# First weights and p in smaller pieces on two DMA queues, a Newton step for 1/f, and the last stores cut otherwise, in a one-core decoder block

## The chip, the cores and the metric

The kernel runs on one core of one Trainium2 chip. A core has five engines that run side by side, each through its own list of instructions in order: TensorE (PE, matmuls; its weight loads are shown apart as PEld), VectorE (DVE), ScalarE (ACT), GpSimd (POOL) and SyncE (SP), which here only issues DMAs. ScalarE issues a few DMAs too. The metric is the device time of one execution in microseconds (us); the kernel before takes 826.49 us in the median of three runs (826.37 to 826.64).

## What is computed

One layer of a decoder block over 256 tokens of 2048 features, in float32. Cut to what matters (weights of a kind in one letter):

```
h  = rmsnorm(x)
u  = h @ w_in                                  # 12288 columns, split into
c, b, xa, za, q, fl, iv, og, ga, gb            # gates and values
ya = b * conv3(c * xa) * silu(za)              # short convolution, 1024 wide
o  = gated recurrence of (silu(q), (1-lb)*sigmoid(-fl), iv, log f), 8 heads of 128
yb = rmsnorm_per_head(o) * silu(og)
m  = sigmoid(ga) * (ya @ w_a) + sigmoid(gb) * (yb @ w_b)
x  = x + m @ w_o
x  = x + sigmoid(rmsnorm(x) @ w_pg) * (p @ w_pp)    # p is 256 x 256
out = rmsnorm(x)
```

## The kernel before, in words

**Matmuls in three parts.** Every large product is done as three matmuls in a fast float32 format: a number is split into a high part (rounded, made by ScalarE) and a low part (the rest, made by VectorE), and high x high, high x low and low x high are summed. `split` does that for weights: ScalarE writes `whi` (L124), VectorE `wlo` (L125). `put` does it for x (L197, L198), and `put_p` for p (L897 the copy to the high part, on VectorE; L898 the low part). All three matmuls are at L945 in `product`.

**Stream of weights.** The weights are one stream of positions. Each position is 128 partitions x 1024 columns (512 KB): two slices of 128 rows, each against 512 output columns. A position gives 12 matmuls: two slices, two halves of the tokens, three parts. The first four positions are the product of p with `w_pp` (groups "PP", one position each, 512 output columns each); then come 16 groups of `w_in` of eight positions, the gates with `w_a` and `w_b`, then `w_o`, and last `w_pg`. The main loop runs over the positions; before the matmuls of a position it splits positions up to three ahead (`LEAD`), loads are issued four further ahead, and after the matmuls it advances the epilogues. Four buffers hold split weights, three hold raw ones of two positions each. Python generators hold the epilogues: each `yield` ends a portion, and the loop runs one portion of each active epilogue per position. Where a portion stands decides the order of instructions on each engine; within an engine nothing overtakes.

**The start.** At L154 the whole of p (256 KB) is loaded on SP's queue. `load_first` (L106 to L111) loads position 0 in two halves of 512 columns, one on ScalarE's queue and one on SP's, and position 1 in one DMA. Then follow the small parameters `prm_t` (L158), and positions 2 to 5 mixed with pieces of x (L810). Ten matmuls on a tile of zeros, which VectorE clears first (L821), run at L825 before any weights are there. In the loop, position 0 is split by halves, each preceded by `put_p` of its 128 rows of p; the first half's six matmuls go high x high, low p, low weights, so that they can begin before the low parts are made. Evictions of the PP groups are at L713, and their stores are put off.

**The recurrence.** `hgrn(j)` runs twice (j = 0, 1; about 100 to 185 us and 300 to 365 us). It builds a decay-masked product of queries and keys by levels of blocks: factors on VectorE, ScalarE (exponentials) and GpSimd, many small matmuls (`products`, L389, and L520), and masked copies (`keep`, copy_predicated) from PSUM into the tiles `both` and `a`. For the innermost level of two rows it makes f = exp(b_r - b_l) on ScalarE (L500) and 1/f by two reciprocals of 256 columns on VectorE (L501, L503), multiplies keys by 1/f on VectorE (L509) and queries by f on GpSimd (L510), and copies `both` into `a` under a mask (L511), twice. Products with the values are at L542 to L544.

**The convolution.** `ep_xa` turns its input through DRAM (`turned`), then for four tiles of features does one scaled copy on ScalarE (L608) and seven fused multiply-adds on VectorE (L617), spread over portions. Its result is used by `ep_b`.

**The end.** The last group of `w_pg` is done by token halves, the last half of tokens in two pieces of 256 columns. After the last matmul come the sigmoid, product, sum and squares (`last_half`, L747 to L752), the norm factor r on GpSimd (L773), the scaling of 2048 columns in four quarters (ScalarE L778, two quarters; VectorE L780 and L782, one each), and a store per quarter (L785; one on ScalarE's queue, three on SP's).

**What orders the work around the change.** SP issues its DMAs in program order, and a DMA waits on a semaphore that is shared with an earlier one (eight in turn). `tc.issue_after` places an instruction behind a named one in its engine's list. Nothing else reorders.

Of the kernel before, what the change touches and what calls it, by code (L numbers as in the profile page):

```python
# [9 lines left out]
F32 = mybir.dt.float32  # L10
# [5 lines left out]
P = 128  # L16
T = 256
# [6 lines left out]
CW = 512  # L24
PLE = 256
EPS = 1e-6
WARM = 10
LB_FLOOR = 1e-30
LB_MAX = 1.0 - 1e-6
SCAN = 64  # L30
# [14 lines left out]
def hybrid_kernel(ctx, tc, xT, x, pT, prm, gfin, masks, w_in, w_a, w_b, w_o, w_pg, w_pp, out):  # L45
# [57 lines left out]
                nc.sync.dma_start(out=raw, in_=w[g, :, c : c + 2, :])  # L103
        return loaded[pos // 2]

    def load_first(pos, queues):  # L106

        w, g, c = stream[pos]
        n = 2 * CW // len(queues)
        for i, eng in enumerate(queues):  # L110
            eng.dma_start(out=load(pos)[:, pos % 2, i * n : (i + 1) * n], in_=w[g, :, c, i * n : (i + 1) * n])  # L111

    def split(pos, halves=(0, 1)):
        w, g, c = stream[pos]
        src = load(pos)[:, pos % 2, :]

        pool, n = (pools["late"], 6) if (pos - state.get("late", len(steps))) % 10 < 6 and "late" in state else (wp, 4)
        if pos not in parts:
            parts[pos] = tuple(
                pool.tile([P, 2 * CW], F32R, tag=tag, bufs=n, name=nm(tag)) for tag in ("whi", "wlo")  # L120
            )
        hi, lo = parts[pos]
        s = slice(halves[0] * CW, (halves[-1] + 1) * CW)
        a = nc.scalar.activation(out=hi[:, s], in_=src[:, s], func=AF.Copy)  # L124
        v = nc.vector.tensor_tensor(  # L125
            out=lo[:, s], in0=src[:, s], in1=hi[:, s].bitcast(F32), op=ALU.subtract
        )
        state["splits"] = (a.ins, v.ins)
# [22 lines left out]
    FIRST = 6  # L151

    praw = t4()[:, : 2 * T]
    nc.sync.dma_start(out=praw.rearrange("p (k t) -> p k t", k=2), in_=pT)  # L154
    load_first(0, (nc.scalar, nc.sync))
    load_first(1, (nc.sync,))
    prm_t = const.tile([P, PRM_N], F32, name="prm_t")
    nc.sync.dma_start(out=prm_t, in_=prm)  # L158

    if PAD_CONST:  # L160
        nc.gpsimd.memset(const.tile([P, PAD_CONST], F32, name="pad"), 0.0)
# [189 lines left out]
    def hgrn(j):  # L351
# [122 lines left out]
        for i in range(4):  # L474
            keep(both, 2 + i, heads(bk), 32 * i)
        Xs.append(level(LEVELS[1]))
        yield
        yield
        yield

        e = t4()
# [10 lines left out]
        nc.vector.tensor_tensor(out=X[:, 0], in0=ev[:, :, 0], in1=kv[:, :, 0], op=ALU.mult)  # L492
        nc.gpsimd.tensor_tensor(out=X[:, 1], in0=ev[:, :, 1], in1=qv[:, :, 1], op=ALU.mult)

        f, rf = (t4()[:, :512] for _ in range(2))
        bl, br = halves(b, 2)
        nc.vector.tensor_tensor(
            out=f.rearrange("p (n c) -> p n c", c=1), in0=br, in1=bl, op=ALU.subtract
        )
        nc.scalar.activation(out=f, in_=f, func=AF.Exp)  # L500
        nc.vector.reciprocal(out=rf[:, :256], in_=f[:, :256])  # L501
        yield
        nc.vector.reciprocal(out=rf[:, 256:], in_=f[:, 256:])  # L503
        yield
        k2, q2 = tiles(kT, 2), tiles(qT, 2)
        fv, rv = (z.rearrange("p (h k n) -> p h k n", h=4, k=2) for z in (f, rf))
        for blk in range(2):
            kk, qq = k2[:, :, blk, :, 1 - blk, 0], q2[:, :, blk, :, 1 - blk, 0]
            nc.vector.tensor_tensor(out=kk, in0=kk, in1=rv[:, :, blk], op=ALU.mult)  # L509
            nc.gpsimd.tensor_tensor(out=qq, in0=qq, in1=fv[:, :, blk], op=ALU.mult)  # L510
            nc.vector.copy_predicated(  # L511
                out=a[:, blk],
                mask=mask_t[:, len(LEVELS) + blk : len(LEVELS) + blk + 1, :].to_broadcast([P, 4, P]), data=both,
            )
        yield
        yield
        bo = bank("s")
# [75 lines left out]
    def ep_xa(j, psum):  # L593
        cx = t4()
        plain_times(psum, state["c", j], cx)
        cxT = yield from turned(cx, 4)
        cv = t4("cv", 1)
        for h in range(2):
            for i in range(2):
                n = h * 2 + i  # L600
                k = j * 4 + n
                d, s = cv[:, n * T : (n + 1) * T], cxT[:, n * T : (n + 1) * T]

                def w(tap):
                    c = PRM_CONV + tap * 8 + k
                    return prm_t[:, c : c + 1]

                nc.scalar.activation(out=d, in_=s, func=AF.Identity, scale=w(2))  # L608

                for tap, to, fr, n_ in (  # L610
                    (1, 1, 0, P - 1), (1, P, P + 1, P - 1), (1, T - 1, P - 1, 1),
                    (0, 2, 0, P - 2), (0, P, P + 2, P - 2), (0, T - 2, P - 1, 1), (0, T - 1, P - 2, 1),
                ):
                    if (tap, to) == (0, 2):
                        yield
                        yield
                    nc.vector.scalar_tensor_tensor(  # L617
                        out=d[:, to : to + n_], in0=s[:, fr : fr + n_], scalar=w(tap), in1=d[:, to : to + n_],
                        op0=ALU.mult, op1=ALU.add,
                    )  # L620
                if n < 3:
                    yield
                    yield
        state["cv", j] = cv

    def ep_za(j, psum):
# [142 lines left out]
    def last_norm(t):  # L769

        xs, r, tot = state["x"], sc(1, "r3", 2), state["tot3", t]
        nc.vector.tensor_tensor(out=tot, in0=tot, in1=state["ss3"][:, t * 6 + 4 : t * 6 + 5], op=ALU.add)
        nc.gpsimd.tensor_tensor(out=r, in0=tot, in1=mhalf[:, :1], op=ALU.pow)  # L773
        for q in (2, 0, 3, 1):
            s = slice(q * CW, (q + 1) * CW)
            d = xs[:, t, s]
            if q < 2:
                nc.scalar.activation(out=d, in_=d, func=AF.Identity, scale=r)  # L778
            elif q == 2:
                nc.vector.tensor_scalar(out=d, in0=d, scalar1=r, scalar2=None, op0=ALU.mult)  # L780
            else:
                nc.vector.scalar_tensor_tensor(  # L782
                    out=d, in0=d, scalar=r, in1=state["gfin"][:, s], op0=ALU.mult, op1=ALU.mult
                )
            (nc.scalar if q == 1 else nc.sync).dma_start(out=out[:, t, s], in_=d)  # L785

    def ep_last(t, halves):

# [24 lines left out]
        )  # L813

    for c in range(4):
        load_first(c + 2, (nc.sync,))
        load_x(c)


    warm = pools["tmp1"].tile([P, 4, P], F32, tag="both", bufs=1, name="warm")  # L820
    nc.vector.memset(warm[:, :2, :], 0.0)  # L821
    warm = warm[:, :2, :].rearrange("p h t -> p (h t)").bitcast(mybir.dt.bfloat16)
    wb = bank("s")
    for _ in range(WARM):
        nc.tensor.matmul(wb, warm[:, :P], warm, start=True, stop=True)  # L825

    def put_x(k):
        put(state["hT"], k, xraw[k // 4][:, (k % 4) * T : (k % 4 + 1) * T], gain(PRM_GMIX, k))
# [119 lines left out]
    for pos, (gi, c) in enumerate(steps[:last_group]):  # L948
# [8 lines left out]

            order.enter_context(tc.issue_after(state["evicted"]))
        while done < min(pos + 1 + ahead(pos), len(steps)):
            if done == 0:  # L960
                for i in range(2):
                    put_p(i)
                    split(done, (i,))
            else:
                for k in range(2 * (done - 4), min(2 * (done - 4) + 2, KT)) if done >= 4 else ():
                    put_x(k)
                split(done)
            done += 1
        order.close()
        if 2 <= pos < 6:  # L970
# [13 lines left out]
        hi, lo = parts.pop(pos)  # L984
        for i in range(2):
            k = 2 * c + i
            s = slice(i * CW, (i + 1) * CW)
            for n in ((0,), (2,), (1,)) if pos == 0 and i == 0 else ((0, 1, 2),):
                for t in range(NT):
                    product(psum[t], state[opname], k, t, hi[:, s], lo[:, s], k == 0, k == 2 * nch - 1, n)  # L990


        if kind == "PG" and j == 0 and c < 2:
# [130 lines left out]
```

## Time and profile before

| | |
|---|---|
| time, median of 3 runs | 826.49 us (826.37 to 826.64) |
| profiled execution, its own time | 827.48 us |
| its span, first to last instruction | 825.0 us |
| TensorE clock granted, mean | 0.996 |
| TensorE busy | 814.1 us, 99% |
| VectorE / ScalarE / GpSimd busy | 533.1 / 431.6 / 86.8 us |
| DMA | 187.25 MB, 227 GB/s mean |
| first useful matmul, first x matmul, last matmul | 5.36, 17.05, 815.67 us |

How to read it: times in the views are microseconds from the start of the span. A row of the timeline gives start, busy time, engine, line, operation, tiles written and read, and in brackets how long the engine stood idle before it and what ended that. A row of the waits gives who waited for whom, the total, how often and the longest. "issue" is idle time for which the profile shows no cause. SPq, ACTq and PEq are the engines' sequencers, which issue DMAs and handle semaphores. The ends of matmuls are modelled, so the distance between starts says more than the busy time.

### The profile page before, as it was taken

The page shows a single profiled execution, that of the slowest core. Times are in us where ns is not written, and L with a number is a line of the kernel's source. Part 1 is how long each engine was busy: PE and PEld are TensorE (multiplying, and loading weights), DVE is VectorE, ACT ScalarE, POOL GpSimd, SP SyncE. Part 2 cuts the span into 40 slices and gives each one's busy share as a digit, 9 for nine tenths or more (in the row PEclk, how much of TensorE's full clock was granted, in tenths as well). Part 3 has the DMA queues.
Part 4 walks back from the last instruction along what each step waited for, and adds up shares of the span by engine and source line. Part 5 has one row for each costly group of instructions (what it writes and reads, how often), then busy time and mean ns, then how long its engine had stood idle before and what let it go on. Part 6 is the DMA issues. An engine that isn't in the chain of part 4 may idle for free.

```text
span 825.0 us, 10664 instructions
## 1 busy us (share of the span) xinstructions
PE 814.1 (99%) x4186; PEld 674.1 (82%) x4186; DVE 533.1 (65%) x616; ACT 431.6 (52%) x555; POOL 86.8 (11%) x74
## 2 busy tenths in 40 slices
PE   9999999999999999999999999999999999999995
PEld 6888888888888888888888888888888888888885
DVE  5747698966766598977645546545544656679633
ACT  7667465455564465466443543544444455566522
POOL 1000045200000064100001001000100000001210
PEclk9999999999999999999999999999999999999998
DMA  9969656648776664748555755756755787887702
GB/s 340 371 262 339 219 189 207 209 154 263 245 235 226 205 205 160 249 155 286 200 185 186 264 187 174 253 202 204 245 182 192 248 293 274 303 301 269 292 1 103
DMA packets 40659, 187.25 MB, mean 227 GB/s; under 512 B 4640, under 2 KB 13856, under 8 KB 22432
## 3 DMA queue, kind: packets, MB, share of 16 engines
q1 hardware_dynamic: 40176, 185.78, 65.8%
q10 hardware_dynamic: 432, 0.79, 0.3%
q8 instruction: 32, 0.52, 0.2%
q14 instruction: 19, 0.16, 0.1%
HBM read 172.92 MB, written 13.63 MB: 226 GB/s over the span
## 4 chain that ended last, share of the span: by engine, by line
PE 96%; issue 1%; DMA 1%; DVE 0%; ACT 0%; SPq 0%; POOLq 0%; POOL 0%
PE g L945 94%; PE s L945 1%; PE s L389 1%; DMA raw<-in_w_pp 1%; PE s L520 0%; PE s L544 0%; PE s L543 0%; PE s L542 0%; ACT xs L778 0%; DVE wlo L125 0%; ACT whi L124 0%; DVE t L748 0%; DVE t L752 0%; DVE xs L751 0%; POOLq L1119 0%
## 5 line engine op out<-in xcount | busy, mean ns | idle before, releaser
L125 DVE TENSOR_TENSOR wlo<-raw,whi 128x1024 fp32r<-128x1024 f32 (+1 forms) x293 | 365.5, 1253 | 252.3 <-ACT whi L124 251.5
L124 ACT ACTIVATE whi<-raw 128x1024 fp32r<-128x1024 f32 (+1 forms) x293 | 307.6, 1056 | 334.4 <-PE g L945 291.9
L945 PE MATMUL g<-whi,xh 128*128 128x512 f32 (+1 forms) x912 | 351.8, 387 | 0.5 <-issue 0.5
L945 PE MATMUL g<-wlo,xh 128*128 128x512 f32 (+1 forms) x912 | 351.9, 386 | 0.0
L945 PE MATMUL g<-whi,xl 128*128 128x512 f32 (+1 forms) x912 | 351.8, 386 | 0.0
L945 PEld LDWEIGHTS g<-whi,xh 128*128 128x128 f32 x912 | 171.4, 188 | 35.0 <-issue 1.0
L945 PEld LDWEIGHTS g<-whi,xl 128*128 128x128 f32 x912 | 171.4, 188 | 34.4
L945 PEld LDWEIGHTS g<-wlo,xh 128*128 128x128 f32 x912 | 171.5, 188 | 34.0
L945 PE MATMUL g<-whi,mh 128*128 128x512 f32 x128 | 49.8, 390 | 0.0
L945 PE MATMUL g<-wlo,mh 128*128 128x512 f32 x128 | 49.7, 390 | 0.0
L945 PE MATMUL g<-whi,ml 128*128 128x512 f32 x128 | 49.6, 390 | 0.0
L672 POOL TENSOR_TENSOR t<-ga,gb 128x512 f32<-128x512 f32 x6 | 10.6, 1788 | 198.1 <-DVE gb L667 198.1
L945 PEld LDWEIGHTS g<-whi,mh 128*128 128x128 f32 x128 | 24.0, 188 | 5.2 <-ACT mh L678 0.3
L945 PEld LDWEIGHTS g<-whi,ml 128*128 128x128 f32 x128 | 24.0, 188 | 5.1 <-DVE ml L679 0.2
L945 PE MATMUL g<-whi,yaTh 128*128 128x512 f32 x72 | 28.1, 395 | 0.0
L945 PE MATMUL g<-wlo,yaTh 128*128 128x512 f32 x72 | 28.0, 391 | 0.1
L945 PEld LDWEIGHTS g<-wlo,mh 128*128 128x128 f32 x128 | 24.0, 188 | 4.9
L945 PE MATMUL g<-whi,yaTl 128*128 128x512 f32 x72 | 27.9, 390 | 0.0
L443 POOL TENSOR_TENSOR t<-b 128x512 f32<-128x512 f32 x10 | 20.4, 2036 | 68.2 <-DVE b L319 41.1
L945 PE MATMUL g<-whi,ybTl 128*128 128x512 f32 x64 | 24.9, 389 | 0.0
L945 PE MATMUL g<-whi,ybTh 128*128 128x512 f32 x64 | 24.9, 389 | 0.0
L945 PE MATMUL g<-wlo,ybTh 128*128 128x512 f32 x64 | 24.9, 389 | 0.0
(156 smaller groups left out, 515.3 us busy)
## 6 DMA issues: line engine op xcount, KB each, us to landing
raw<-in_w_in SPq DMA_DIRECT2D x93, 1024.0 KB, 5.0
raw<-in_w_o SPq DMA_DIRECT2D x16, 1024.0 KB, 5.3
raw<-in_w_pg SPq DMA_DIRECT2D x16, 1024.0 KB, 5.8
turn<-t SPq DMA_DIRECT2D x72, 128.0 KB, 2.6
t<-turn SPq DMA_DIRECT2D x18, 512.0 KB, 5.1
raw<-in_w_a SPq DMA_DIRECT2D x8, 1024.0 KB, 5.2
raw<-in_w_b SPq DMA_DIRECT2D x8, 1024.0 KB, 5.1
raw<-in_w_in SPq DMA_DIRECT2D x6, 512.0 KB, 7.8
```

The costliest lines, as they stand in the source:

```text
L124: a = nc.scalar.activation(out=hi[:, s], in_=src[:, s], func=AF.Copy)
L125: v = nc.vector.tensor_tensor(out=lo[:, s], in0=src[:, s], in1=hi[:, s].bitcast(F32), op=ALU.subtract)
L389: nc.tensor.matmul(heads(bk)[r, h, c if at is None else slice(at, at + 32)], key(h)[:, r], query(h)[:, c], start=True, stop=True, tile_pos ...
L443: nc.gpsimd.tensor_tensor(out=er, in0=br, in1=ref, op=ALU.subtract)
L672: (nc.vector if j == 3 else nc.gpsimd).tensor_tensor(out=spread(m, t), in0=blocks(ga[:, s]), in1=blocks(gb[:, s]), op=ALU.add)
L945: nc.tensor.matmul(psum, a, b, start=first and n == 0, stop=last and n == 2)
```

## The change

It does six things.

1. p's two tiles are loaded by a DMA each (128 KB): the first on SP's queue, the second on ScalarE's.
2. Position 0's first 512 columns come as two pieces of 256 columns on ScalarE's queue, ahead of p's second tile; the other 512 columns on SP's; position 1 as two halves on SP's. `prm_t` is loaded later, behind position 2. The splits follow these pieces (`EARLY`), the first half's matmuls run by 256 columns, and `put_p` of the second tile is placed behind the splits of the first two pieces.
3. The warm-up matmuls are 7 and not 10, on a constant of ones that exists already, so VectorE clears no tile for them.
4. In `hgrn`, 1/f is no reciprocal any more: ScalarE makes exp(-(b_r - b_l)), and VectorE improves it by one Newton step, r (2 - f r), in a product and a fused operation with the sign reversed; the sign is put right where the keys are multiplied. The two masked copies of `both` into `a` move to earlier portions.
5. In `ep_xa` two portions more pass before the convolution, and fewer between its tiles.
6. In `last_norm` VectorE scales 256, 512 and 256 columns and not 512 and 512; SP stores 256, 512 and 512 columns, ScalarE one piece of 768.

On TensorE the order of everything behind the first six matmuls is as before. There are 3 pairs of weight load and matmul fewer (warm-ups) and 6 pairs more (the pieces), and two instructions more that wait for a second semaphore.

The diff, cut to its core:

```
@@ -24,7 +24,9 @@
 CW = 512
 PLE = 256
 EPS = 1e-6
-WARM = 10
+WARM = 7
+EARLY = {0: ((0, CW // 2), (CW // 2, CW), (CW, 2 * CW)), 1: ((0, CW), (CW, 2 * CW))}
 LB_FLOOR = 1e-30
 LB_MAX = 1.0 - 1e-6
 SCAN = 64
@@ -103,14 +105,7 @@
                 nc.sync.dma_start(out=raw, in_=w[g, :, c : c + 2, :])
         return loaded[pos // 2]
 
-    def load_first(pos, queues):
-        w, g, c = stream[pos]
-        n = 2 * CW // len(queues)
-        for i, eng in enumerate(queues):
-            eng.dma_start(out=load(pos)[:, pos % 2, i * n : (i + 1) * n], in_=w[g, :, c, i * n : (i + 1) * n])
-    def split(pos, halves=(0, 1)):
+    def split(pos, c0=0, c1=2 * CW):
         w, g, c = stream[pos]
         src = load(pos)[:, pos % 2, :]
 
@@ -120,7 +115,7 @@
                 pool.tile([P, 2 * CW], F32R, tag=tag, bufs=n, name=nm(tag)) for tag in ("whi", "wlo")
             )
         hi, lo = parts[pos]
-        s = slice(halves[0] * CW, (halves[-1] + 1) * CW)
+        s = slice(c0, c1)
         a = nc.scalar.activation(out=hi[:, s], in_=src[:, s], func=AF.Copy)
         v = nc.vector.tensor_tensor(
             out=lo[:, s], in0=src[:, s], in1=hi[:, s].bitcast(F32), op=ALU.subtract
@@ -151,11 +146,22 @@
     FIRST = 6
 
     praw = t4()[:, : 2 * T]
-    nc.sync.dma_start(out=praw.rearrange("p (k t) -> p k t", k=2), in_=pT)
-    load_first(0, (nc.scalar, nc.sync))
-    load_first(1, (nc.sync,))
+    def load_p(k, eng=nc.sync):
+        eng.dma_start(out=praw[:, k * T : (k + 1) * T], in_=pT[:, k, :])
+    def load_columns(pos, c0, c1, eng):
+        w, g, c = stream[pos]
+        eng.dma_start(out=load(pos)[:, pos % 2, c0:c1], in_=w[g, :, c, c0:c1])
+    load_p(0)
+    load_columns(0, 0, CW // 2, nc.scalar)
+    load_columns(0, CW // 2, CW, nc.scalar)
+    load_p(1, nc.scalar)
+    load_columns(0, CW, 2 * CW, nc.sync)
+    for n in range(2):
+        load_columns(1, n * CW, (n + 1) * CW, nc.sync)
     prm_t = const.tile([P, PRM_N], F32, name="prm_t")
-    nc.sync.dma_start(out=prm_t, in_=prm)
 
     if PAD_CONST:
         nc.gpsimd.memset(const.tile([P, PAD_CONST], F32, name="pad"), 0.0)
@@ -474,8 +480,9 @@
         for i in range(4):
             keep(both, 2 + i, heads(bk), 32 * i)
         Xs.append(level(LEVELS[1]))
-        yield
-        yield
+        for blk in range(2):
+            yield
+            keep(a[:, blk], len(LEVELS) + blk, both)
         yield
 
         e = t4()
@@ -492,26 +499,27 @@
         nc.vector.tensor_tensor(out=X[:, 0], in0=ev[:, :, 0], in1=kv[:, :, 0], op=ALU.mult)
         nc.gpsimd.tensor_tensor(out=X[:, 1], in0=ev[:, :, 1], in1=qv[:, :, 1], op=ALU.mult)
 
-        f, rf = (t4()[:, :512] for _ in range(2))
+        fr, one = t4(), t4()[:, :512]
+        f, rf = fr[:, :512], fr[:, 512:]
         bl, br = halves(b, 2)
         nc.vector.tensor_tensor(
             out=f.rearrange("p (n c) -> p n c", c=1), in0=br, in1=bl, op=ALU.subtract
         )
+        nc.scalar.activation(out=rf, in_=f, func=AF.Exp, scale=-1.0)
         nc.scalar.activation(out=f, in_=f, func=AF.Exp)
-        nc.vector.reciprocal(out=rf[:, :256], in_=f[:, :256])
-        yield
-        nc.vector.reciprocal(out=rf[:, 256:], in_=f[:, 256:])
+        yield
+        nc.vector.tensor_tensor(out=one, in0=f, in1=rf, op=ALU.mult)
+        nc.vector.scalar_tensor_tensor(out=rf, in0=one, scalar=2.0, in1=rf, op0=ALU.subtract, op1=ALU.mult)
         yield
         k2, q2 = tiles(kT, 2), tiles(qT, 2)
         fv, rv = (z.rearrange("p (h k n) -> p h k n", h=4, k=2) for z in (f, rf))
         for blk in range(2):
             kk, qq = k2[:, :, blk, :, 1 - blk, 0], q2[:, :, blk, :, 1 - blk, 0]
-            nc.vector.tensor_tensor(out=kk, in0=kk, in1=rv[:, :, blk], op=ALU.mult)
+            nc.vector.scalar_tensor_tensor(
+                out=kk, in0=kk, scalar=-1.0, in1=rv[:, :, blk], op0=ALU.mult, op1=ALU.mult
+            )
             nc.gpsimd.tensor_tensor(out=qq, in0=qq, in1=fv[:, :, blk], op=ALU.mult)
-            nc.vector.copy_predicated(
-                out=a[:, blk],
-                mask=mask_t[:, len(LEVELS) + blk : len(LEVELS) + blk + 1, :].to_broadcast([P, 4, P]), data=both,
-            )
         yield
         yield
         bo = bank("s")
@@ -594,6 +602,8 @@
         cx = t4()
         plain_times(psum, state["c", j], cx)
         cxT = yield from turned(cx, 4)
+        yield
+        yield
         cv = t4("cv", 1)
         for h in range(2):
             for i in range(2):
@@ -620,7 +630,8 @@
                     )
                 if n < 3:
                     yield
-                    yield
+                    if n < 1:
+                        yield
         state["cv", j] = cv
 
     def ep_za(j, psum):
@@ -771,18 +782,25 @@
         xs, r, tot = state["x"], sc(1, "r3", 2), state["tot3", t]
         nc.vector.tensor_tensor(out=tot, in0=tot, in1=state["ss3"][:, t * 6 + 4 : t * 6 + 5], op=ALU.add)
         nc.gpsimd.tensor_tensor(out=r, in0=tot, in1=mhalf[:, :1], op=ALU.pow)
-        for q in (2, 0, 3, 1):
-            s = slice(q * CW, (q + 1) * CW)
-            d = xs[:, t, s]
-            if q < 2:
+        def scale(eng, c0, c1):
+            d = xs[:, t, c0:c1]
+            if eng is nc.scalar:
                 nc.scalar.activation(out=d, in_=d, func=AF.Identity, scale=r)
-            elif q == 2:
+            elif c0 < 3 * CW:
                 nc.vector.tensor_scalar(out=d, in0=d, scalar1=r, scalar2=None, op0=ALU.mult)
             else:
                 nc.vector.scalar_tensor_tensor(
-                    out=d, in0=d, scalar=r, in1=state["gfin"][:, s], op0=ALU.mult, op1=ALU.mult
+                    out=d, in0=d, scalar=r, in1=state["gfin"][:, c0:c1], op0=ALU.mult, op1=ALU.mult
                 )
-            (nc.scalar if q == 1 else nc.sync).dma_start(out=out[:, t, s], in_=d)
+        for queue, *pieces in (
+            (nc.sync, (nc.vector, 1280, 1536)), (nc.sync, (nc.scalar, 0, 512)), (nc.sync, (nc.vector, 1536, 2048)),
+            (nc.scalar, (nc.scalar, 512, 1024), (nc.vector, 1024, 1280)),
+        ):
+            for eng, c0, c1 in pieces:
+                scale(eng, c0, c1)
+            queue.dma_start(out=out[:, t, pieces[0][1] : c1], in_=xs[:, t, pieces[0][1] : c1])
 
     def ep_last(t, halves):
 
@@ -813,16 +831,16 @@
         )
 
     for c in range(4):
-        load_first(c + 2, (nc.sync,))
+        load_columns(c + 2, 0, 2 * CW, nc.sync)
+        if c == 0:
+            nc.sync.dma_start(out=prm_t, in_=prm)
         load_x(c)
 
 
-    warm = pools["tmp1"].tile([P, 4, P], F32, tag="both", bufs=1, name="warm")
-    nc.vector.memset(warm[:, :2, :], 0.0)
-    warm = warm[:, :2, :].rearrange("p h t -> p (h t)").bitcast(mybir.dt.bfloat16)
+    ones = [nc.const_aps.tensor(1.0, [P, n], mybir.dt.bfloat16) for n in (P, CW)]
     wb = bank("s")
     for _ in range(WARM):
-        nc.tensor.matmul(wb, warm[:, :P], warm, start=True, stop=True)
+        nc.tensor.matmul(wb, *ones, start=True, stop=True)
 
     def put_x(k):
         put(state["hT"], k, xraw[k // 4][:, (k % 4) * T : (k % 4 + 1) * T], gain(PRM_GMIX, k))
@@ -957,14 +975,17 @@
 
             order.enter_context(tc.issue_after(state["evicted"]))
         while done < min(pos + 1 + ahead(pos), len(steps)):
-            if done == 0:
-                for i in range(2):
-                    put_p(i)
-                    split(done, (i,))
-            else:
+            for c0, c1 in EARLY.get(done, ((0, 2 * CW),)):
+                if done == 0 and c0 % CW == 0:
+                    with ExitStack() as first:
+                        for i in state["splits"] if c0 else ():
+                            first.enter_context(tc.issue_after(i))
+                        put_p(c0 // CW)
                 for k in range(2 * (done - 4), min(2 * (done - 4) + 2, KT)) if done >= 4 else ():
                     put_x(k)
-                split(done)
+                split(done, c0, c1)
             done += 1
         order.close()
         if 2 <= pos < 6:
@@ -984,10 +1005,13 @@
         hi, lo = parts.pop(pos)
         for i in range(2):
             k = 2 * c + i
-            s = slice(i * CW, (i + 1) * CW)
-            for n in ((0,), (2,), (1,)) if pos == 0 and i == 0 else ((0, 1, 2),):
-                for t in range(NT):
-                    product(psum[t], state[opname], k, t, hi[:, s], lo[:, s], k == 0, k == 2 * nch - 1, n)
+            for c0, c1 in EARLY[0][:2] if pos == 0 and i == 0 else ((0, CW),):
+                s = slice(i * CW + c0, i * CW + c1)
+                for n in ((0,), (2,), (1,)) if pos == 0 and i == 0 else ((0, 1, 2),):
+                    for t in range(NT):
+                        product(
+                            psum[t][:, c0:c1], state[opname], k, t, hi[:, s], lo[:, s], k == 0 and c0 == 0, k == 2 * nch - 1, n
+                        )
 
 
         if kind == "PG" and j == 0 and c < 2:
```

## The prediction, as it was made before the result was known

> **What bounds it now.** I read the engines' busy times first, then who waited for whom, then the first 17 us and the last 9 us instruction by instruction, because the first two leave nothing else. The page, section 1:
>
> ```profile
> PE 814.1 (99%) x4186; PEld 674.1 (82%) x4186; DVE 533.1 (65%) x616; ACT 431.6 (52%) x555; POOL 86.8 (11%) x74
> ```
>
> The waits of TensorE (PE), in all 825 us:
>
> ```profile
> PE s L825 <- DVE warm L821: 1.2, 1, 1.2
> PE g L945 <- issue: 0.5, 1, 0.5
> ```
>
> and of its weight loads (PEld), of which these two are at the start:
>
> ```profile
> PEld g L945 <- ACT whi L124: 0.6, 1, 0.6
> PEld g L945 <- DVE wlo L125: 0.5, 1, 0.5
> ```
>
> So matmuls set the time: in the plateau one of 512 columns starts every 0.227 us, and from 9.55 us to 815.7 us nothing but the "issue" hole and hand-overs of 0.1 to 0.2 us interrupts them. Only three places can change the time: the start, that hole, the tail. The start, from the timeline (start us, us busy; the bracket is the idle time before and its cause):
>
> ```profile
> 1.19 4.45 PE L825 MATMUL s<-warm 128*128 128x512 bf16 x10 [1.19 <-DVE warm L821]
> 4.48 0.49 DVE L897 CAST yaTh<-t 128x256 fp32r<-128x256 f32 x2 [3.35 <-DMA t<-in_pT]
> 4.68 1.17 ACT L124 ACTIVATE whi<-raw 128x512 fp32r<-128x512 f32 x2 [2.01 <-DMA raw<-in_w_pp]
> 6.83 1.06 ACT L124 ACTIVATE whi<-raw 128x1024 fp32r<-128x1024 f32 x1 [0.98 <-DMA raw<-in_w_pp]
> 9.21 0.19 PEld L945 LDWEIGHTS g<-wlo,yaTh 128*128 128x128 f32 x1 [0.52 <-DVE wlo L125]
> 17.05 0.39 PE L945 MATMUL g<-whi,xh 128*128 128x512 f32 x1
> ```
>
> The first useful matmul starts at 5.36; the four projection groups of 12 matmuls end when the first x matmul starts, at 17.05. At 0.227 us the 48 need 10.9 us; 11.7 pass. The difference is a slow beginning (the ten warm-ups come every 0.43 us, and so do the first useful ones until about 6.0) and the wait for step 1's low part at 9.21.
>
> **Start: gain 0.9 us, between 0.2 and 1.1.** Before, the first half of the weights (256 KB) and p (256 KB) land 3.9 and 3.7 us after their issue at 0.74, in parallel on two queues. After, the first need is 128 KB of each. The two queues had moved some 220 KB by 3.0 us (55 and 166 GB/s in the second and third us), then go at about 390 GB/s; 256 KB less is up to 0.66 us earlier, so p's tile at 3.8, the piece at 4.0. If the slow beginning counts descriptors (128 per DMA both ways) and not bytes, nothing is won: that is the other end. The high part of 256 columns is 0.41 us (0.63 for 512, 1.06 for 1024, a straight line): first useful matmul at about 4.5. Its twelve matmuls of 256 columns (0.118 us each at full pace, from the 256-column matmuls at 804 to 815 us; 0.21 at half pace) end near 6.6. p's second tile is third on ScalarE's queue; the queues share the engines, so it lands at 4.9 (equal bytes) to 5.9 us (equal descriptors); I take 5.5. Then on VectorE, by the rows of before: CAST 0.29, low part of 512 columns 0.69, low part of p 0.42, to 6.97. The second half runs 6.6 to 8.0. Step 1's halves land with the old 6.83 as the last; low parts are done at about 7.5 and 8.7, before they are needed, so the 9.21 wait goes. Then 36 x 0.227 = 8.2: first x matmul at 16.2 instead of 17.05.
>
> What is late next: step 2. Its weights land at 8.4, its low part was ready at 10.76 and used at 11.84: 1.08 us of slack, and 1.5 in steps 3 to 7, where ScalarE works without a pause. A gain over 1.1 us is eaten there. Costs that I put at nothing: three DMA issues of 0.40 us on ScalarE's queue push its table load (1.28) from 1.17 to about 2.0; it ends by 3.5, before the first piece lands. Uncovered it would cost what it overruns. prm moves behind step 2's weights; it is 36 KB and first used at 12.66. The warm-ups lose VectorE's memset (0.27) and start at about 0.85.
>
> [...]
>
> **Middle, the reciprocal and the masks: 0.** In each half (j = 0, 1) VectorE loses two reciprocals (1.74 + 1.69) and gains a product of 512 (0.71, row L484) and a fused one (0.74, row L782); two more are fused at the same 0.42. That is 2.0 us less, and ScalarE has one exponential more (0.62). Two masked copies (0.75 each) move 5 to 10 us earlier. The convolution starts two steps later, then goes faster. None of it is on the path: the low parts around 140 to 190 us are ready 5.0 to 8.5 us before TensorE uses them, the four masked-product operands were ready at 162.4 and first read at about 164.5. The new wait of GpSimd's product with f stands ahead of one more product and the memset of a, nothing else. If a 5 us delay came, TensorE would start to pay one for one; I see no such delay.
>
> **The issue hole: 0 taken, between -0.7 and +0.9.** TensorE stands 0.93 us between two matmuls that need nothing new:
>
> ```profile
> 166.48 0.39 PE L945 MATMUL g<-whi,xl 128*128 128x512 f32 x1
> 167.41 0.50 PE L945 MATMUL g<-whi,xh 128*128 128x512 f32 x1 [0.54 <-issue]
> ```
>
> The page shows an instruction queue (q8, 32 packets, 0.52 MB): 8372 matmuls and weight loads in 32 packets are about 260 instructions each. One of these packets moves at 165.0 to 166.0, the next at 169.0. The 160 tiny masked matmuls at 162.8 to 165.2 eat 320 instructions in 2.4 us, so TensorE runs out of code. The change adds about 8 TensorE instructions ahead of it (3 warm-up pairs fewer, 6 matmul pairs and 2 waits more), so the packet's end comes four full matmuls, 0.9 us, earlier in the work, while its fetch begins only 0.1 us earlier: +0.8. Against that, fetches are not regular (139.0 and 145.2 are 6 us apart), the second half (344 us) has the same tiny matmuls and no hole, and one profile does not say that the timed runs have it. I take no change and leave both ends in the range.
>
> **Tail: gain 0.2 us, between -0.2 and +0.3.**
>
> ```profile
> 818.12 0.55 POOL L773 TENSOR_TENSOR r<-tot,mhalf 128x1 f32<-128x1 f32 x1 [9.89 <-DVE tot L772]
> 818.71 0.49 DVE L780 TENSOR_SCALAR xs<-xs,r 128x512 f32<-128x512 f32 x1 [0.67 <-POOL r L773]
> 819.22 1.55 SPq L785 DMA_DIRECT2D out<-xs  x3
> 820.07 0.34 ACTq L785 DMA_DIRECT2D out<-xs  x1
> ```
>
> The four stores (1 MB) move without a break at 370 to 390 GB/s from 820.1 to 822.8; the rest is fixed. With 256 columns first (about 0.28 us instead of 0.49) the first store leaves 0.2 us earlier, and the stream with it. ScalarE's last store grows to 384 KB but leaves at the same 820.07, with its third VectorE part done at about 819.95; if it moved alone at the end, it would cost 0.2.
>
> **Sum.** The profiled execution took 827.48 us: a span of 825.00 and 2.48 around it. The sum -0.9 + 0 + 0 - 0.2 = -1.1 brings it to 826.4. The median of the timed runs is 826.49, 0.99 below the profiled one; the same -1.1 gives **825.4**.
>
> **Rivals.** (A) The code hole grows by 0.8: 826.2. For it: the count of instructions. Against it: the irregular fetches. 0.17. (B) The hole goes (-0.7), and the start gives its full 1.1: -2.0, 824.5. For it: the hole stands in one of two like places. 0.24. (C) Slower: seven warm-ups at 0.43 end at about 3.85, the first weights come at 4.5, and the pause keeps the clock at half pace. Before, TensorE was never idle until it sped up at about 6.0. If the speed-up comes some 3.4 us later, at 9.4, the 48 matmuls go at 0.427 until then: 4.5 to 9.4 is 11.5 of them, the other 36.5 take 8.3, first x matmul at 17.7 instead of 17.05. That is +0.65 - 0.2: 826.9; another such step of 3.4 us later, 828.5. It decides if the pause exceeds what the gate forgives. Against it: at the end matmuls stop at 815.7 and the granted clock (0.63 over 816 to 825 us) falls only about 2.5 us later. 0.10. [...] (D) The change does not do what it says: the first DMAs are limited by descriptors, pieces land as the old halves did, and only the 9.21 wait goes: -0.3, 826.2. 0.09. My forecast: 0.40, itself 824.8 to 826.0.
>
> The range 824.4 to 826.9 leaves out the far half of C and little else. A measurement of this kernel can tell about 0.2% (1.65 us) from no change, so faster means below 824.84: B and the lower edge of the forecast, 0.28; slower, above 828.14: C's two steps or a stall not seen, 0.07; the rest 0.65.
>
> **What would show it.** First matmul of L945's successor line near 4.5, no wait near 9.2, first x matmul near 16.2; step 2's low part just in time. The hole at 166 us: same, longer by about four matmuls, or gone. The first store issued near 819.0. Warm-up spacing of 0.43 past 6.0 us would be C; first pieces landing after 4.4, D. Any TensorE wait between 140 and 190 us on a, kT or qT would make the middle wrong.

## The result, and the profile after

The kernel after takes **827.52 us** (median of 16 runs, 826.68 to 830.57), the kernel before on the same chip 826.42 (16 runs, 826.23 to 827.42): ratio 1.0022 [1.0013, 1.0031] (the ratio counts every run and lies near that of the means; the medians alone are 1.0013 apart). The forecast was 825.4, its range ended at 826.9. The 16 runs do not lie in one group: nine are 826.68 to 827.53 with a granted clock of 0.996 to 0.998, seven are 828.75 to 830.57 at 0.993 or 0.994. The profiled execution is one of the seven: 830.16, a span of 828.4 and 1.8 around it.

Page, section 1, kernel after; TensorE's sum is 1.4 us up, with matmuls at half pace in it, and its share is down to 98%, so the loss is idle time and clock:

```profile
PE 815.5 (98%) x4189; PEld 675.3 (82%) x4189; DVE 531.6 (64%) x619; ACT 433.4 (52%) x559; POOL 90.6 (11%) x74
```

The waits of TensorE in the whole span (us in total, times, longest). The wait at 9.21 for step 1's low part is gone; a new one, for p's high part, has come, and the "issue" hole is still there:

```profile
PE g L963 <- DVE yaTh L915: 1.6, 1, 1.6
PE g L963 <- issue: 0.9, 1, 0.9
PE s L843 <- PEq L1137: 0.8, 1, 0.8
```

The start, from the timeline of the kernel after (start us, us busy; bracket: idle time before and its cause):

```profile
0.77 3.15 PE L843 MATMUL s<-const-bfloat16-1.0 128*128 128x512 bf16 x7 [0.77 <-PEq L1137]
...
3.33 0.29 DVE L915 CAST yaTh<-t 128x256 fp32r<-128x256 f32 x1 [3.33 <-DMA t<-in_pT]
...
4.00 0.80 PE L963 MATMUL g<-whi,yaTh 128*128 128x256 f32 x2
...
7.90 0.29 DVE L915 CAST yaTh<-t 128x256 fp32r<-128x256 f32 x1 [1.77 <-DMA t<-in_pT]
...
8.34 0.47 PE L963 MATMUL g<-whi,yaTh 128*128 128x512 f32 x1 [1.64 <-DVE yaTh L915]
```

The first useful matmul starts at 4.00 instead of 5.36, even earlier than forecast. But p's second tile is copied at 7.90, and TensorE stands until 8.34. Then it goes on at half pace: the table by stages (us, then busy us and count by engine, near the end PEclk, the granted clock) has nine matmuls in the 3.4 us from 9.0, where the kernel before does fifteen (second row):

```profile
9.00:12.40 3.40, 3.40 (x9) 2.62 (x10) 2.56 (x4) 2.01 (x2) 0.00 (x0) 0.51 1.04 403
```

```profile
9.00:12.40 3.40, 3.31 (x15) 2.66 (x15) 1.94 (x3) 2.15 (x4) 0.00 (x0) 1.00 1.02 366
```

(That column is 1.00 ahead of the first clock event, too, where the warm-ups come every 0.427 us: for the start, read the spacing.) The first x matmul comes at 19.89 instead of 17.05. The hole, from the chain of waits (start us, us, what), and the end, from the timeline:

```profile
168.10 0.66 PE g L963 x2
168.76 0.93 issue
169.69 10.72 PE g L963 x46
```

```profile
821.23 0.56 POOL L784 TENSOR_TENSOR r<-tot,mhalf 128x1 f32<-128x1 f32 x1 [9.89 <-DVE tot L783]
821.82 0.35 DVE L790 TENSOR_SCALAR xs<-xs,r 128x256 f32<-128x256 f32 x1 [0.67 <-POOL r L784]
...
822.20 1.56 SPq L803 DMA_DIRECT2D out<-xs  x3
```

**Where the time went**, profiled execution against profiled execution: first x matmul +2.84; from there to the last matmul +0.27 (798.62 to 798.89 us); from the last matmul to the end +0.27; around the span -0.70 (2.48 to 1.78). Together +2.68, which is 830.16 - 827.48. The clock record of the trace says full pace from 5.54, half from 8.95, full from 12.36; in the kernel before, full from 6.00 without a break.

### The profile page after: what moved, and what is told of

Same layout as the page of the kernel before. It is cut to its first block, busy times and chain, and to the rows that moved or that the text cites. A ratio compares the mean times of both kernels' runs of the same rounds, so it can differ in the third digit from the quotient of the medians.

```text
span 828.4 us, 10685 instructions
## 1 busy us (share of the span) xinstructions
PE 815.5 (98%) x4189; PEld 675.3 (82%) x4189; DVE 531.6 (64%) x619; ACT 433.4 (52%) x559; POOL 90.6 (11%) x74
## 4 chain that ended last, share of the span: by engine, by line
PE 96%; issue 1%; DMA 1%; DVE 0%; ACT 0%; ACTq 0%; POOLq 0%; POOL 0%
PE g L963 94%; DMA t<-in_pT 1%; PE s L963 1%; PE s L395 1%; PE s L528 0%; PE s L551 0%; PE s L552 0%; PE s L550 0%; ACT xs L788 0%; ACTq L155 0%; DVE t L759 0%; DVE t L763 0%; DVE xs L762 0%; POOLq L1143 0%; POOL r L784 0%
## 5 line engine op out<-in xcount | busy, mean ns | idle before, releaser
L963 PE MATMUL g<-whi,yaTh 128*128 128x512 f32 (+1 forms) x74 | 29.1, 398 | 1.8 <-DVE yaTh L915 1.6
L963 PE MATMUL g<-wlo,yaTh 128*128 128x512 f32 (+1 forms) x74 | 29.1, 398 | 0.0
L963 PE MATMUL g<-whi,yaTl 128*128 128x512 f32 (+1 forms) x74 | 29.0, 396 | 0.0
```

Source lines behind the costliest of these rows:

```text
L963: nc.tensor.matmul(psum, a, b, start=first and n == 0, stop=last and n == 2)
```

## Experiments

Every kernel ran beside the kernel before, whose median was 826.59 to 826.73 on the four chips used. **Theory L**: p's second tile is late, the pause costs its length and a piece of half clock. **Theory W**: seven warm-ups end too early. **Theory H**: more TensorE instructions lengthen the code hole. The rival to all: the Newton step, the masks or the tail did it.

### Which part

Three kernels: before with the edits of the start alone (DMAs, pieces, EARLY, warm-ups); with those of the middle alone (Newton step, masks, portions); with those of the tail alone.

> The kernel before with the edits of the start alone (pieces, queues, p's tiles, 7 warm-ups). Theory 1 (p's second tile lands late and TensorE pauses 1.8 us, after which the clock is at half pace for 3.4 us in some executions): the loss of the whole change is here, +0.5 to +1.5 us in the median, with times in two groups some 3 us apart, and the wait for p's second tile near 8 us in the trace. Theory 2 (the loss comes from the recurrence and the code hole in the middle): 0 to -1 us here, no second group. Theory 3 (tail): as theory 2.

> The kernel before with the Newton step, the moved masked copies and the moved portions of the convolution alone. Theory 1: 0 within 0.3 us, one group of times, and the hole at 166 us where it was, since the number of TensorE instructions ahead of it is that of before. Theory 2: +0.5 us or more.

> The kernel before with the stores cut otherwise alone. The prediction: -0.2 us, first store 0.2 us earlier. Theory 3 (the larger last store and the smaller first one lose more than the earlier start gains): +0.2 to +0.4 us.

Start alone **827.75**, ratio 1.0011 [1.0002, 1.0020], up to 829.76; middle alone 826.34, 0.9994 [0.9985, 1.0003]; tail alone 826.61, 0.9997 [0.9988, 1.0006]. The loss is in the start; middle and tail make no difference that can be measured. The two groups that theory 1 expected of the first are not there: nine of its eleven runs lie between 827.27 and 828.13, and two at 828.92 and 829.76. The traced run is the one at 829.76; it has the pause (6.00 to 7.69) and half clock from 8.69 to 12.10, as the kernel after.

### p's second tile

p by one DMA of 256 KB, first on SP's queue:

```diff
-    load_p(0)
+    nc.sync.dma_start(out=praw.rearrange("p (k t) -> p k t", k=2), in_=pT)
...
-    load_p(1, nc.scalar)
```

> The changed kernel with p loaded by one DMA of 256 KB, first on SP's queue, as before; all else changed. Theory 1: no pause for p, one group of times, and at least 1 us faster than the changed kernel's median, 825.3 to 826.3 us; first x matmul at 16.3 to 16.8 us. Theories 2 and 3: the time stays at +1 us over before, though the wait for p goes.

**827.66**, 1.0006 [0.9997, 1.0015], in two groups: four runs at 826.04 to 826.74, six at 827.5 to 828.1, one at 829.37. I had expected 825.3 to 826.3. The pause is gone from the trace, and so are the runs at 830, as L says; but the median is no lower than that of the kernel after, and a later group stays, so L is not all. The profiled run is the fastest one: after 7 warm-ups TensorE is idle for 0.76 us, and yet the clock happened to be full from 4.00:

```profile
0.77 3.15 PE L842 MATMUL s<-const-bfloat16-1.0 128*128 128x512 bf16 x7 [0.77 <-PEq L1136]
4.68 0.50 PE L962 MATMUL g<-whi,yaTh 128*128 128x256 f32 x2 [0.76 <-ACT whi L119]
```

### Warm-ups

The kernel before with `WARM = 7`; the kernel after with `WARM = 10`; p whole with `WARM = 10`; the kernel after with the pause filled:

```diff
             k = 2 * c + i
+            if pos == 0 and i == 1:
+                for _ in range(8):
+                    nc.tensor.matmul(wb, *ones, start=True, stop=True)
```

> The kernel before with 7 warm-ups in place of 10, nothing else. Warm-ups then end at about 1.19 + 7 x 0.427 = 4.2 us, and the first useful matmul still comes at 5.36, after 1.2 us of idle. Late-p theory (all the loss is the pause for p's second tile): there is no such pause here, so the time stays at the kernel before's, within 0.3 us. Warm-up theory (idle time between the warm-ups and the first weights puts the speed-up of the clock one 3.4 us window later in some executions): part of the runs, or all, come 1.0 to 2 us later (each useful matmul of a window at half pace loses 0.2 us, 8 to 15 of them), the trace has 0.427 us spacing beyond 6.0 us, up to 9.4. Code-hole reckoning: 6 TensorE instructions fewer, so the hole at 166 us, if there, comes three matmuls later (after 9 matmuls of the step in place of 6) and is shorter by up to 0.7.

> The kernel after with 10 warm-ups in place of 7. They end at 0.77 + 10 x 0.427 = 5.0, so the first useful matmuls come at 5.0 instead of 4.0, and the pause for p's second tile shrinks from 1.9 to about 0.9 us; the work behind p still starts at about 8.3. Warm-up theory: the slow group (828.7 to 830.6) goes, median 826.5 or less. Late-p theory: whatever is behind 8.3 stays there; the time stays at 827.5 if the shorter pause still costs a window at half pace, and falls to 826.5 only if a pause of 0.9 us doesn't. The trace decides: half pace behind the pause (late p) or before it (warm-ups). Code hole: 6 instructions more, so three matmuls earlier than the kernel after's, into the tiny masked matmuls; 0.4 longer by the reckoning with instructions.

> The kernel after with p by one DMA first on SP's queue and 10 warm-ups. Neither the pause for p's second tile nor idle time between warm-ups and first weights. Both theories together: one group of runs only, at the fast group of the kernel with p whole and 7 warm-ups, 826.0 to 826.2 less nothing: median 826.1. Late-p theory alone: same distribution as with p whole and 7 warm-ups, two groups, median 827.7. Warm-up theory alone says one group, too, so this run tells whether the second group there came from the warm-ups.

> The kernel after with 8 dummy matmuls of 512 columns put between position 0's first 256 columns and its second 256, so that TensorE works on (8 x 0.227 = 1.8 us) where it waits for p's second tile now. The work behind the pause starts as before at 8.3. Late-p theory with the clock's answer: no half pace from 8.95 to 12.36, the runs at 830 go, median 826.5. If the loss is the pause's length alone (1.9 us, not the clock): no change, 827.5. If the late speed-up comes from the early end of the warm-ups: both groups stay as they are, at 827.0 and 829 to 830, and the dummies themselves run at 0.427 in some executions, adding up to 1.5.

**Before with 7: 827.55**, 1.0010 [1.0001, 1.0018], spread over 825.81 to 828.76. In its trace the clock is full only from 9.82, where the kernel before has 6.00; nine matmuls stand in the 3.4 us ahead of that (third row), and the first x matmul comes at 18.52:

```profile
1.19 3.17 PE L825 MATMUL s<-warm 128*128 128x512 bf16 x7 [1.19 <-DVE warm L821]
5.48 1.22 PE L945 MATMUL g<-whi,yaTh 128*128 128x512 f32 x2 [1.13 <-ACT whi L124]
```

```profile
6.40:9.80 3.40, 3.40 (x9) 2.63 (x9) 2.39 (x4) 2.12 (x2) 0.00 (x0) 1.00 1.02 388
```

W holds in this execution: 1.13 us of idle behind the seventh warm-up were enough to lose 3.4 us at full pace. The runs at 825.81 and 825.95, below every run of the kernel before beside them (826.17 and up), will hardly have lost as much; neither of them was traced. **After with 10: 827.93**, 1.0021 [1.0012, 1.0031], still with three runs at 830.5 to 831.4. The traced run is one of the three; it has the pause even longer (2.28 us, p's second tile took 7.0 us), and half clock from 9.07 to 12.49. So it is the pause, not the warm-ups, that makes that group. **p whole with 10: 827.29**, 1.0008 [1.0000, 1.0017], and one group at last (826.83 to 827.80), which W said; but 1.2 above what I expected, for which neither L nor W has a reason. Its waits name it:

```profile
PE s L394 <- issue: 1.3, 1, 1.3
```

**Pause filled: 828.25**, 1.0024 [1.0015, 1.0034], all eight runs between 827.85 and 829.55. The clock stayed full from 4.90, so it was the idle time that brought it down, and no run is at 830; the median did not follow. (The dummies stand ahead of position 0's second slice of 128 rows; two of the eight ran at 3.71, ahead of all useful matmuls.) Its traced run, 827.92, has a span 1.12 us longer than that of the kernel before: the first x matmul comes 0.38 later (17.43), the hole has grown by 0.42 (to 1.12), and the end behind the last matmul is 0.32 longer.

### The hole

I then counted TensorE's matmuls, weight loads and waits, and the drain at its start, in the order of every trace. The hole, where there is one, comes in **every** kernel behind number **1985**, whatever that instruction is, and ends 2.37 to 2.47 us after the start of a packet of the instruction queue (2.70 and 2.84 in two). So more instructions ahead move the stop to earlier work. The direct test is the kernel before, its warm-ups cut finer, same length in time:

```diff
-    for _ in range(WARM):
-        nc.tensor.matmul(wb, warm[:, :P], warm, start=True, stop=True)
+    for n in 7 * [CW] + 10 * [160]:
+        nc.tensor.matmul(wb[:, :n], warm[:, :P], warm[:, :n], start=True, stop=True)
```

> The kernel before, its 10 warm-ups of 512 columns put as 7 of 512 and 10 of 160: 5200 columns instead of 5120, the same length, 14 TensorE instructions more, nothing else moved. Code-hole theory (in every trace so far that has the hole, TensorE stops behind its instruction number 1985, and goes on 2.4 us after the start of a code packet; more instructions ahead bring number 1985 earlier in the work, and the packet comes hardly earlier): the hole comes seven matmuls earlier, at the end of the tiny masked matmuls (about 148.0 us behind the first x matmul, where it was 149.4), and is 0.9 to 1.3 us; the time rises by 0.5 to 0.8 to 827.2 to 827.4. Rival (the longer hole of the last kernels belongs to their start, to the Newton step or to chance): hole as in the kernel before, 0 to 0.7, time 826.5 to 826.8.

**829.99** (five runs, 828.11 to 830.10), 1.0034 [1.0022, 1.0047]: 14 instructions that do nothing cost 3.3 us in the median, by the ratio 1.8 to 3.9. The place was as expected, at the end of the masked matmuls; the size was far beyond it, since the hole grew to 2.0 us and brought the clock down as well. Timeline and stages of this kernel:

```profile
164.42 0.74 PE L389 MATMUL s<-qT,kT 128*32 128x32 f32 x63
167.00 0.22 PE L389 MATMUL s<-qT,kT 128*32 128x32 f32 x1 [1.84 <-issue]
...
168.78 0.63 PE L945 MATMUL g<-whi,xh 128*128 128x512 f32 x1
```

```profile
168.50:172.00 3.50, 3.50 (x10) 2.73 (x9) 0.00 (x0) 0.36 (x1) 0.00 (x0) 0.52 0.04 14
172.00:300.00 128.00, 128.00 (x578) 106.43 (x577) 87.03 (x111) 73.95 (x102) 9.41 (x8) 1.00 0.65 218
```

All traces in one table. "More" is the number of TensorE instructions ahead of the masked matmuls, against the kernel before; the hole is the idle time beyond the normal spacing; the stream is the time from the first x matmul to the last matmul:

```
kernel                  more    hole  stream  stream - hole
before, 7 warm-ups        -6    none  797.94  797.94
before                     0    0.70  798.62  797.92
middle only                0    none  797.85  797.85
tail only                  0    0.43  798.30  797.87
no pieces                 +1    none  797.73  797.73
old loads                 +1    none  797.88  797.88
after                     +8    1.10  798.89  797.79
start only                +8    1.38  799.36  797.98
p whole                   +8    0.56  798.38  797.82
after, 10 warm-ups       +14    1.11  798.94  797.83
p whole, 10 warm-ups     +14    1.51  799.34  797.83
p2 on SP, 10 warm-ups    +14    1.95  799.69  797.74
before, finer warm-ups   +14    2.01  801.34  799.33 (half clock: 1.6 of it)
pause filled             +23    1.12  799.04  797.92
```

Without the hole, and in the one kernel without the half clock, all streams are 797.7 to 798.0: the whole body of the kernel, Newton step or not, is the same. The hole is 0.19 on average in the five rows at 0 or +1 and the one at -6, 1.01 at +8 (three traces), 1.54 from +14 on (five). The scatter in a row is that of the packet's start, which comes 1.0 to 2.2 us after the first masked matmul; what sets it was not found.

### Taking the losses out

p's second tile second on SP's queue, with `WARM = 10`; then also position 0's first 512 columns in one piece of 256 KB, 12 instructions fewer; then the old loads (p whole, step 1 in one DMA) with 10 warm-ups on the constant and the rest of the kernel after:

```diff
     load_p(0)
-    load_columns(0, 0, CW // 2, nc.scalar)
-    load_columns(0, CW // 2, CW, nc.scalar)
-    load_p(1, nc.scalar)
+    load_columns(0, 0, CW, nc.scalar)
+    load_p(1)
```

(This is the second kernel, whose EARLY has (0, CW) in place of the two pieces; the first keeps the pieces and moves `load_p(1)` alone, the third loads p and step 1 as the kernel before.)

> The kernel after with p's second tile moved from third place on ScalarE's queue to second place on SP's (still a DMA of its own) and 10 warm-ups. Queue-place theory (the tile is late because its descriptors of 2 KB stand behind two of 1 KB each on a queue that shares the engines with SP's large ones): it lands by about 5, no pause of TensorE at 6.4 to 8.3, the clock stays full once it is, all runs in one group at 827.0 to 827.4 as with p whole (the hole with 14 instructions more is in it). Rival (a DMA of 128 KB for p by itself, or any third DMA of the start, trickles): the pause stays, runs of 828 to 831.

> What is left when both losses are taken out: the kernel after, but position 0's first 512 columns in one piece of 256 KB on ScalarE's queue (as in the kernel before, so 12 instructions fewer), p's tiles one behind the other on SP's queue, 10 warm-ups on the constant. TensorE's number of instructions ahead of the masked matmuls is that of the kernel before. Theory (start by warm-ups, hole by count): no pause, one group of runs, hole at 149.4 behind the first x matmul and 0 to 0.7 long as in the kernel before, first x matmul at about 16.6 to 16.8 (no wait for step 1's low part): 826.0 to 826.2, 0.4 to 0.6 below the kernel before. If the hole doesn't go by the count: 826.8 to 827.2.

> The loads of the kernel before (p whole, position 0's halves on two queues, step 1 in one piece and one low part) with what else the kernel after has: 10 warm-ups on the constant (from 0.77 instead of 1.19 us, no memset on VectorE), the parameters behind step 2, Newton step, portions, tail. TensorE's instructions ahead of the masked matmuls are those of the kernel before or two fewer (no wait for the memset). Theory (hole by count, start by warm-ups and loads): first useful matmul at 5.2 to 5.4 and first x matmul at 16.6 to 17.1, one group of runs, hole 0 to 0.7 at 149.4 behind the first x matmul: 825.9 to 826.4, at or below the kernel with p's tiles on SP's queue (826.3). If the pieces and the halves of step 1 were what made that kernel fast: 826.6 to 827.0.

**p2 on SP: 827.17**, 1.0003 [0.9994, 1.0013], one group (826.18 to 827.83). TensorE no longer waits for p; waits of 0.41 and 0.23 us are left, for position 0's second half. Against the kernel after with 10 warm-ups (827.93, three runs over 830) one line of the program has moved, so the late tile is what made those runs. The DMA issues on the pages (KB each, us from issue to landing), the kernel after first, this one second:

```profile
t<-in_pT SPq DMA_DIRECT2D x1, 128.0 KB, 2.6
...
t<-in_pT ACTq DMA_DIRECT2D x1, 128.0 KB, 6.2
```

```profile
t<-in_pT SPq DMA_DIRECT2D x2, 128.0 KB, 2.7
```

The same 128 KB land 2.7 us after issue from second place on SP's queue, 6.2 from third place on ScalarE's. In the other three kernels that leave the tile there it took 5.3 (pause filled), 5.6 (start only) and 7.0 us (after with 10), so its landing varies, too. Whether it is the queue or the place in it that does this was not separated; the tile's packets are of 1 KB, as those of the pieces, not of 2 KB as I had expected. **No pieces: 826.29**, 0.9993 [0.9985, 1.0002]; no hole, as the count said. Its first x matmul came at 17.53, where I had expected 16.6 to 16.8: now position 0's second half, behind both tiles of p, is late. **Old loads: 826.23**, 0.9993 [0.9984, 1.0002], one group (825.72 to 826.69), no hole; its first useful matmul came at 5.63, not at 5.2 to 5.4, for it waited for the high part of its weights:

```profile
PE s L840 <- PEq L1134: 0.8, 1, 0.8
PE g L960 <- ACT whi L119: 0.5, 1, 0.5
```

Both are what the kernel before is, within what can be measured: their medians are 0.4 and 0.5 below it, where that of the kernel after is 1.1 above.

## Why the prediction was wrong, point by point

- **Start, -0.9: wrong, the step that failed is "I take 5.5" for p's second tile.** The pieces did as said, or better (first useful matmul 4.00 against 4.5). The tile landed at 7.9 (issue at 1.66, 6.2 us), 2 us beyond my later end of 5.9; its last packet of data ended at 7.46. In the trace the DMA ends in 16 parts, one by one: by the closing packets eleven of them were done by 5.6, the other five between 6.6 and 7.6, and VectorE's copy starts only behind the last. While the tile's packets ran, from 4.4 to 7.5, SP's queue moved 0.8 MB (the packets of SP's queue took 75%, those of ScalarE's 15% of the time of the 16 DMA engines). I had bounded a mean; what TensorE waits for is the last one. The sum: it went on at 8.34 instead of 6.6, +1.7; a window of 3.41 us at 0.427 instead of 0.227 per matmul, +1.6; hand-overs, +0.35. That is 19.89 instead of 16.2.
- **What the trace seemed to say of the clock: misread.** I held against rival C that the clock fell only 2.5 us after the last matmul, as if the gate forgave that long. In all fourteen traces it falls 2.3 to 5.5 us after the start of the last matmul, a spread of nearly one window: where the windows lie decides most of it. No trace stood behind the step of 3.4 us when C reckoned with it; the runs show it: half pace from 8.95 to 12.36 in the kernel after and from 9.07 to 12.49 in after with 10, 3.41 and 3.42 us. C's mechanism is real (before with 7 warm-ups: full from 9.82 instead of 6.00 in its trace), though what hit the kernel after was the other pause, which I had not priced.
- **What idle time did to the clock.** Four pauses that lay within one window brought the clock down for 3.41 us: 1.58 (start only), 1.80 (after), 2.01 (finer warm-ups) and 2.44 us (after with 10; all beyond the normal spacing, and all but 0.1 us of each within). Holes of 1.51 and 1.95 us that a window's end cut in two (1.28 + 0.23, 0.48 + 1.47) did not, nor did 1.12. The length of the one pause is not what decides, though: in the window with the last matmul as much as 1.99 us of idle left the clock full. I estimate the idle time of each window of the fourteen traces from the starts of the matmuls, as what their distance exceeds the plateau's (0.227 us per 512 columns, 0.427 at half pace). From full pace the clock fell in every window with 2.01 us or more (the four pauses come to 2.01 to 2.41 with the smaller waits beside them) and in none with 1.99 or less. It rose behind windows with at most 0.54 us idle, and not behind 0.86 (tail only) or 1.50 (before with 7). So 1.13 us behind the warm-ups lost a window, where a hole of 1.12 us at full pace cost its length alone. By a window I mean one of the stretches of 3.413 us that the clock events mark out: those of the kernel after at 5.54, 8.95, 12.36 and 821.32 are whole multiples of 3.413 us apart (1, 1 and 237 of them), as are those of the kernel before at 6.00 and 818.38 (238).
- **Issue hole, 0 taken: wrong, and rival A right in the mean.** "Fetches are not regular" is true of each trace, not of the mean: 1.01 - 0.19 = +0.8 for eight instructions, which is A's number and its reason. (Three traces against six; between the two profiled runs of before and after it is 1.10 - 0.70 = +0.4.) The stop was four matmuls earlier, as A had it. The second half has the same masked matmuls and no hole: number 1985 lies far ahead of them. Why TensorE stops at this number and at no later one stays open.
- **Middle, 0: right.** Streams without the hole agree to 0.3 us, and TensorE waits for none of a, kT, qT.
- **Tail, -0.2: not borne out.** The first store leaves 0.97 instead of 1.10 us after r begins, 0.13 gained; the span still ends 7.15 instead of 6.88 us after it. The tail alone measured -0.1, with an interval of 0.7 either way. The fourteen traces say more: from the start of the last matmul to the end of the span it is 9.26 to 9.33 us in the five with the old tail and 8.95 to 9.72 in the nine with the new one, 9.39 on average against 9.29. What makes the new tail scatter was not found.
- **Sum.** The forecast needed the start's gain and no cost elsewhere. The nine runs of the earlier group are 0.3 to 1.1 above the kernel before; the pause's length and the hole are enough for that, but none of the nine was traced, and the split stays open. So does the later group of "p whole" (827.5 to 828.1): a window lost at the start fits its size, and is not shown.

## What to carry to other kernels

A DMA that the bottleneck waits for has landed when the slowest of its parts has (here eleven of sixteen by 5.6, the last at 7.6): bound its landing by the last packet, and mind its place: the same tile took 2.7 us second on SP's queue and 5.3 to 7.0 third on ScalarE's. Idle time of 2 us in TensorE (2.01 to 2.41 in four traces) cost its length and, where it fell within one window of 3.41 us, 1.6 us more at half pace, so an early start that is followed by a pause can lose more than it gained. Count instructions, too, where a trace shows such a stop behind a run of tiny ones: eight more, far ahead of it, cost 0.8 us here, on the average of few traces.

## What the runs showed of the hardware

- In all ten traces with a hole TensorE stops behind its recorded instruction 1985, and 14 dummy instructions ahead of it cost 3.3 us in the median. The instruction queue's packets are 16 KB; the trace of the kernel after has 33 of them for 8396 recorded matmuls, weight loads and waits of TensorE, 254 a packet. What lies at number 1985 no run shows.
- p's second tile, third on ScalarE's queue, took 5.3 to 7.0 us in four kernels, and 2.7 second on SP's. The kernel after with 10 warm-ups takes 827.93 with it there and 827.17 with it on SP's; queue and place were not told apart.
